# A group mix done with seven products of block sums instead of eight plain products, on Trainium2

## The chip, the core and the metric

The kernel runs on one core of a Trainium2 chip. In the profile PE is the matrix engine (a matmul streams a moving operand of up to 128x512 against a stationary 128x128 operand), PEld the loading of that stationary operand, DVE the vector engine, ACT the scalar engine, POOL the general engine, and SP the engine that issues most transfers. Each engine works through its own instructions in the order in which they stand in the program, and they wait for one another through semaphores. The metric is the device time in microseconds (us), the median of several runs.

## What is computed

One layer of a bidirectional encoder, 1024 tokens of 2048 channels in float32: a normed and modulated input, one combined projection, windowed attention and a pooling branch side by side, each gated, then merged and projected out. The part at issue is the pooling branch. Its 1024 channels fall into four groups of 256; group g averages over a centred window of 2, 4, 8 or 16 tokens, subtracts the token, and is mapped by a 256x256 matrix of its own:

```python
for gi, w in enumerate(POOL_SIZES):                       # 2, 4, 8, 16
    outs.append((cs[:, hi, gi] - cs[:, lo, gi]) / cnt - ug[:, :, gi])
pooled = jnp.stack(outs, axis=2)
mixed = jnp.einsum('bsgc,gcd->bsgd', pooled, w_grp)       # 256x256 per group
y_p = mixed * scale * silu(gate_p)
```

## The kernel before, in words

Every float32 operand is split into a rounded high part (`hi`, written by ACT, line 96) and the rest (`lo`, written by DVE, line 97). A product is then three matmuls: hi with hi, hi with lo, lo with hi. The split is the work that a product asks of ACT and DVE before PE can start.

The large projections use seven products of block sums for a 2x2 block multiplication, in place of eight (`strassen`, line 212). A pair is one such unit: 256 output channels by 1024 tokens. Its seven products are called by their moving operands B11, T3, T2, B21, T4, T1, B22, and they accumulate in three banks X, V and Z: B11 starts X, which ACT copies into Z (line 293); T3 starts V, and DVE reads V into a tile `p` as soon as T3 has ended; T2 and later T1 and B22 add to Z; B21 adds to X; T4 adds to V. A product is 12 matmuls (line 237): four contraction blocks with `whi` and the high moving part, four with `whi` and the low one, four with `wlo`. `whi` and `wlo` are the split weights, four buffers each, made fresh for each product out of a `raw` tile that a transfer brings. DVE also makes the weight sums in `raw` and `ws`, and adds `part` tiles, which hold an earlier half of the sum and are fetched from DRAM.

A pair is a generator of seven steps. `run` (line 347) and `next_pair` (line 1293) walk through it, and at the steps named in `every` they call one entry of a queue `side`. So the pooling branch is recorded between the steps of nine pairs, and its instructions stand among those of the projections. The order written down this way is an input of a scheduler, which then fixes the order of each engine's instructions by its own estimates, except for those that are pinned with `keep`. PE may hence take matmuls of the next product before the last four of the one that it is in.

In the pooling branch `window` (line 1461) works on 128 channels: it loads `u`, adds shifted copies (one to four times, over 1025 to 1039 columns, tiles `win`), corrects the columns at the two edges one by one (line 1478: 1, 3, 7 or 15 of them), forms the mean minus the token over 1024 columns (line 1480), and splits the result into `phi` and `plo`. `mix` (line 1489) makes 128 output channels: two banks of 512 tokens with 6 matmuls each (lines 1509 to 1511), each read out by DVE with scale and gate (line 1512). For each group the queue holds two windows and two mixes; with one first fetch this makes 17 entries, called at the steps 2 and 5 of nine pairs. A group's weights are split once, in 512 columns (`wgh`, `wgl`).

## Time and profile before

| | |
|---|---|
| median of 3 runs | 2086.41 us (2085.77 to 2087.27) |
| the profiled execution's own time | 2088.67 us |
| its span in the profile | 2086.9 us |
| PE, DVE, ACT busy | 2070.1, 1556.7, 1111.0 us (99%, 75%, 53%) |
| first and last transfer of `u` issued | 1190.4 and 1320.2 us |
| first and last matmul of the mixes | 1229.4 and 1376.5 us |

The span is that of one execution. It is 1.8 us shorter than that execution's own time, which was 2.3 us above the median. A row of the timeline gives the start, the length, the engine, the line, and what is written from what; an instruction can start before the one ahead of it has ended, so the distance from start to start says how long the engine is held, and not the length. A group's row gives its count, its busy time, the mean length of one, and the idle time in front of it.

### The profile page before, as it was taken

The page shows a single profiled execution, that of the slowest core. Times are in us where ns is not written, and L with a number is a line of the kernel's source. Part 1 is how long each engine was busy: PE and PEld are TensorE (multiplying, and loading weights), DVE is VectorE, ACT ScalarE, POOL GpSimd, SP SyncE. Part 2 cuts the span into 40 slices and gives each one's busy share as a digit, 9 for nine tenths or more (in the row PEclk, how much of TensorE's full clock was granted, in tenths as well). Part 3 has the DMA queues.
Part 4 walks back from the last instruction along what each step waited for, and adds up shares of the span by engine and source line. Part 5 has one row for each costly group of instructions (what it writes and reads, how often), then busy time and mean ns, then how long its engine had stood idle before and what let it go on. Part 6 is the DMA issues. An engine that isn't in the chain of part 4 may idle for free.

```text
span 2086.9 us, 29056 instructions
## 1 busy us (share of the span) xinstructions
PE 2070.1 (99%) x9524; PEld 1702.2 (82%) x9524; DVE 1556.7 (75%) x2805; ACT 1111.0 (53%) x2121; POOL 42.6 (2%) x143
## 2 busy tenths in 40 slices
PE   8999999999999999999999999999999999999998
PEld 6678887888888888888888888888888788888886
DVE  5889677776565876777777688857867977889667
ACT  5764444444564634666665444334645644767554
POOL 1100000001000000000000000010000000000000
PEclk9999999999999999999999999999999999999999
DMA  9978877887675477645554576675754566786897
GB/s 343 355 270 267 282 240 245 282 284 223 198 232 170 156 250 258 208 164 174 182 170 149 186 233 222 208 239 187 232 175 158 176 201 202 225 305 207 297 334 247
DMA packets 303393, 476.62 MB, mean 228 GB/s; under 512 B 24322, under 2 KB 140650, under 8 KB 303240
## 3 DMA queue, kind: packets, MB, share of 16 engines
q1 hardware_dynamic: 297616, 459.89, 67.2%
q0 software_dynamic: 4560, 12.75, 1.6%
q10 hardware_dynamic: 1064, 2.11, 0.3%
q8 instruction: 75, 1.23, 0.3%
q14 instruction: 78, 0.64, 0.1%
HBM read 346.70 MB, written 130.05 MB: 228 GB/s over the span
## 4 chain that ended last, share of the span: by engine, by line
PE 91%; DMA 4%; DVE 3%; ACT 1%; issue 1%; SPq 0%; DVEq 0%; ACTq 0%; POOL 0%; POOLq 0%
PE Z L237 30%; PE V L237 20%; PE X L237 20%; PE Z L1686 2%; PE Z L1688 2%; PE Z L1687 2%; PE PB L822 1%; PE X L1686 1%; PE X L1687 1%; PE X L1688 1%; PE V L1687 1%; PE V L1686 1%; PE V L1688 1%; DMA raw<-in_w_in_dram 1%; PE PT L1396 1%
## 5 line engine op out<-in xcount | busy, mean ns | idle before, releaser
L96 ACT ACTIVATE whi<-raw 128x512 fp32r<-128x512 f32 (+1 forms) x528 | 314.7, 600 | 482.8 <-PE Z L237 235.2
L97 DVE TENSOR_TENSOR wlo<-raw,whi 128x512 fp32r<-128x512 f32 (+1 forms) x528 | 339.7, 649 | 144.5 <-PE Z L237 110.9
L97 DVE TENSOR_TENSOR wlo<-wr,whi 128x512 fp32r<-128x512 f32 x224 | 150.7, 689 | 51.5 <-ACT whi L96 46.0
L96 ACT ACTIVATE whi<-wr 128x512 fp32r<-128x512 f32 x224 | 138.2, 628 | 86.9 <-DVE wlo L97 29.8
L103 DVE TENSOR_TENSOR raw<-raw,raw 128x512 f32<-128x512 f32 x76 | 52.5, 690 | 92.7 <-DMA raw<-in_w_merge_dram 62.6
L96 ACT ACTIVATE whi<-ws 128x512 fp32r<-128x512 f32 (+1 forms) x88 | 53.0, 602 | 72.2 <-PE X L237 60.8
L237 PE MATMUL Z<-B22h,whi 128*128 128x512 f32 x328 | 89.9, 392 | 0.0
L237 PE MATMUL Z<-T2h,wlo 128*128 128x512 f32 x328 | 88.9, 390 | 0.8 <-DVE wlo L97 0.8
L237 PE MATMUL Z<-T1h,whi 128*128 128x512 f32 x328 | 89.6, 390 | 0.0
L237 PE MATMUL X<-B11h,whi 128*128 128x512 f32 x328 | 89.5, 391 | 0.0
L237 PE MATMUL X<-B21h,whi 128*128 128x512 f32 x328 | 89.5, 391 | 0.0
L237 PE MATMUL V<-T3h,whi 128*128 128x512 f32 x328 | 89.4, 391 | 0.0
L237 PE MATMUL V<-T4h,whi 128*128 128x512 f32 x328 | 89.3, 391 | 0.0
L237 PE MATMUL Z<-T2h,whi 128*128 128x512 f32 x328 | 89.0, 390 | 0.3 <-ACT Z L293 0.2
L237 PE MATMUL X<-B11l,whi 128*128 128x512 f32 x328 | 89.2, 390 | 0.0
L237 PE MATMUL Z<-T1l,whi 128*128 128x512 f32 x328 | 89.0, 390 | 0.0
L237 PE MATMUL Z<-B22l,whi 128*128 128x512 f32 x328 | 88.9, 390 | 0.0
L237 PE MATMUL V<-T3l,whi 128*128 128x512 f32 x328 | 88.9, 390 | 0.0
L237 PE MATMUL X<-B21l,whi 128*128 128x512 f32 x328 | 88.8, 390 | 0.0
L237 PE MATMUL V<-T4h,wlo 128*128 128x512 f32 x328 | 88.8, 390 | 0.0
L237 PE MATMUL X<-B11h,wlo 128*128 128x512 f32 x328 | 88.8, 390 | 0.0
L237 PE MATMUL V<-T4l,whi 128*128 128x512 f32 x328 | 88.8, 390 | 0.0
(421 smaller groups left out, 4908.7 us busy)
## 6 DMA issues: line engine op xcount, KB each, us to landing
part<-part_d SPq DMA_DIRECT2D x136, 256.0 KB, 5.0
ada<-in_w_ada_dram SPq DMA_DIRECT2D x128, 256.0 KB, 5.4
raw<-in_w_merge_dram SPq DMA_DIRECT2D x64, 512.0 KB, 5.4
wr<-ws_dS SPq DMA_DIRECT2D x60, 512.0 KB, 5.4
raw<-in_w_in_dram SPq DMA_DIRECT2D x56, 512.0 KB, 4.1
wr<-in_w_out_dram SPq DMA_DIRECT2D x48, 512.0 KB, 5.0
proj_d<-part SPq DMA_DIRECT2D x68, 256.0 KB, 2.3
sw<-in_w_out_dram SPq DMA_DIRECT2D x64, 256.0 KB, 4.9
```

Source lines behind the costliest of these rows:

```text
L96: ins = (nc.scalar.activation(hi, src, AF.Copy), nc.vector.tensor_tensor(lo, src, f32(hi), ALU.subtract))
L97: nc.vector.tensor_tensor(lo, src, f32(hi), ALU.subtract))
L103: return (eng or nc.vector).tensor_tensor(o, a, b, ALU.add)
L237: nc.tensor.matmul(ps, w_[:, i], op[mov][j][m_], start=fresh and i == 0 and n == 0, stop=i == nj - 1 and n == 2, skip_group_check=True)
L822: keep(nc.tensor.matmul(opened[i, blk], w[:, kh, nt * P:(nt + 1) * P], mov[kh][m], start=j == n == 0, stop=j == 1 and n == 5, skip_group_c ...
L1396: nc.tensor.transpose(pt[:, i * P:(i + 1) * P], p[:, i * P:(i + 1) * P], ident)
L1686: nc.tensor.matmul(pb, hi, w[0], start=first, stop=False, skip_group_check=True)
L1687: nc.tensor.matmul(pb, lo, w[0], start=False, stop=False, skip_group_check=True)
L1688: nc.tensor.matmul(pb, hi, w[1], start=False, stop=last, skip_group_check=True)
```

## The change

The mix of a group becomes a 2x2 block multiplication with seven products, as the pairs have it. The two windows of a group give the four blocks of 128 channels by 512 tokens, the group's matrix four blocks of 128x128. Each product is three matmuls (hi-hi, hi-lo, lo-hi), so a group has 21 where it had 24. DVE makes the sums of the blocks and of the weights, each product has operands split for it alone (512 columns for `phi` and `plo`, 128 for `wgh` and `wgl`), ACT copies three banks per group, and two more additions join the results. X and V are taken from the banks called "at", Z from those called "sc". Since products add to a bank that ACT has written, two matmuls open these banks once (`open_banks`).

The steps of a group are now: its first window and its fetches (called at the end of the group before), then `window` of the second half with `first`, then `second`, `third`, `fourth`, `fifth`. That makes 21 entries over the same nine pairs, at the steps (2, 5), (1, 3, 5), (2, 5) in turn.

```diff
-            u = pp.tile([P, S + 2 * PAD], F32, tag="u", name=f"u{i}")
+            u = pp.tile([P, S + 2 * PAD], F32, tag="u", name=f"u{i}", bufs=2)
...
-            nc.vector.scalar_tensor_tensor(win, win, 1.0 / w, u[:, PAD:PAD + S],
-                                           op0=ALU.mult, op1=ALU.subtract)
-            hi = pp.tile([P, S], F32R, tag="phi", name=f"phi{i}", bufs=2)
-            lo = pp.tile([P, S], F32R, tag="plo", name=f"plo{i}", bufs=2)
-            split(hi, lo, win)
-            pooled[i] = (hi, lo)
+            nc.vector.scalar_tensor_tensor(mid_, win, 1.0 / w, mid_, op0=ALU.mult, op1=ALU.subtract)
+            blocks[j] = mid_[:, 0:512], mid_[:, 512:1024]
-        def mix(g, j):
...
-            for s in range(2):
-                sl = slice(s * 512, (s + 1) * 512)
-                ps = bank("at")
-                for k in range(2):
-                    hi, lo = pooled[2 * g + k]
-                    nc.tensor.matmul(ps, gh[:, k, wn], hi[:, sl], start=k == 0, stop=False)
-                    nc.tensor.matmul(ps, gh[:, k, wn], lo[:, sl], start=False, stop=False)
-                    nc.tensor.matmul(ps, gl[:, k, wn], hi[:, sl], start=False, stop=k == 1)
...
+            def operand(name, src):
+                ops[name] = [pp.tile([P, 512], F32R, tag=t, name=uid(t), bufs=4) for t in ("phi", "plo")]
+                split(*ops[name], src)
+            def weight(name, src):
+                wts[name] = [pp.tile([P, P], F32R, tag=t, name=uid(t), bufs=3) for t in ("wgh", "wgl")]
+                split(*wts[name], src)
+            def product(name, to, fresh=False):
+                (wh, wl), (mh, ml) = wts.pop(name), ops.pop(name)
+                for n, (w_, m_) in enumerate(((wh, mh), (wh, ml), (wl, mh))):
+                    nc.tensor.matmul(banks[to], w_, m_, start=fresh and n == 0, stop=n == 2, skip_group_check=True)
...
+            def first():
+                (b11, b12), (b21, b22) = blocks[0], blocks[1]
+                st["a"] = a11, a21, a12, a22 = [st["raw"][:, kh, n * P:(n + 1) * P] for kh in range(2) for n in range(2)]
+                sub(b12, b12, b11)
+                t2, st["p7"] = spare("t2")
+                st["u2"], _ = spare("u2")
+                sub(t2, b22, b12)
+                operand("B11", b11)
+                weight("B11", a11)
+                sub(b11, t2, b11)
+                operand("T3", b11)
+                s3 = pp.tile([P, P], F32, tag="wgs", name=uid("wgs"))
+                sub(s3, a11, a21)
+                weight("T3", s3)
+                add(a21, a21, a22)
+                sub(a11, a21, a11)
+            def second():
+                product("B11", "X", True)
+                nc.scalar.activation(banks["Z"], banks["X"], AF.Copy)
+                weight("T2", a11)
+                operand("T2", t2)
+                product("T3", "V", True)
+                nc.scalar.activation(st["p7"], banks["V"], AF.Copy)
+                weight("B21", a12)
+                operand("B21", b21)
+                sub(b21, b21, t2)
...
+            def third():
...
+                product("T2", "Z")
+                nc.scalar.activation(st["u2"], banks["Z"], AF.Copy)
...
+                product("B21", "X")
+                result("11", banks["X"])
...
+            def fourth():
...
+                product("T4", "V")
+                add(st["u2"], banks["V"], st["u2"])
+                result("21", st["u2"])
+                product("T1", "Z")
+                add(st["p7"], banks["Z"], st["p7"])
+                result("22", st["p7"])
...
+            def fifth():
+                product("B22", "Z")
+                result("12", banks["Z"])
+                for n, sg in enumerate(st["sg"]):
+                    store(yp_d[(2 * g + n) * P:(2 * g + n + 1) * P, :], sg)
+                then()
+        def open_banks():
+            hi = op["B11"][0][0]
+            for _ in range(2):
+                nc.tensor.matmul(bank("sc", "OPEN"), hi[:, 0:P], hi, start=True, stop=True)
...
-        while side:
-            next_pair((2, 5))
+        for n in range(9):
+            next_pair((1, 3, 5) if n % 3 == 1 else (2, 5))
```

The change leaves the instructions of the projections as they are, but the scheduler places them anew among those of the mixes. Three places follow. In the names a number marks the buffer; a name that comes back with the same number is the same tile.

The first place is PE in the last group (window 16), where the pair's product B22 adds to Z. Before, the twelve matmuls stand together; these are the last two with the high weights and the four with `wlo`, and the next product follows:

```order
L237 MATMUL Z_13084<-B22l_7073,whi_13323 128x512
L237 MATMUL Z_13084<-B22l_7077,whi_13323 128x512
L237 MATMUL Z_13084<-B22h_7064,wlo_13324 128x512
L237 MATMUL Z_13084<-B22h_7068,wlo_13324 128x512
L237 MATMUL Z_13084<-B22h_7072,wlo_13324 128x512
L237 MATMUL Z_13084<-B22h_7076,wlo_13324 128x512
L237 MATMUL Z_13284<-T2h_6899,whi_13375 128x512
```

With the change the same place reads:

```order
L237 MATMUL Z_13250<-B22l_7073,whi_13548 128x512
L237 MATMUL Z_13250<-B22l_7077,whi_13548 128x512
L1503 MATMUL X_13587<-phi_13527,wgh_13531 128x512
L1503 MATMUL X_13587<-plo_13528,wgh_13531 128x512
L1503 MATMUL X_13587<-phi_13527,wgl_13532 128x512
L237 MATMUL Z_13250<-B22h_7064,wlo_13549 128x512
L237 MATMUL Z_13250<-B22h_7068,wlo_13549 128x512
L237 MATMUL Z_13250<-B22h_7072,wlo_13549 128x512
L237 MATMUL Z_13250<-B22h_7076,wlo_13549 128x512
L237 MATMUL Z_13456<-T2h_6899,whi_13568 128x512
```

A product of the group's mix (line 1503) now stands between the eight matmuls with the high weights and the four that need `wlo_13549`.

The second place is DVE at the same point. Before, from the last windowing additions on (V_13085 is the bank that T4 has just added to, V_13285 that of the next pair's T3):

```order
L103 TENSOR_TENSOR win_8_13351<-win_4_13349 128x1025
L103 TENSOR_TENSOR u_2651_13179<-V_13085,u_2651_13179 128x512
L97 TENSOR_TENSOR wlo_13324<-raw_13073,whi_13323 128x512
L1478 TENSOR_SCALAR win_8_13351<-win_8_13351 128x1 x15
L106 TENSOR_TENSOR raw_13271<-raw_13271 128x4x128
L1480 SCALAR_TENSOR_TENSOR win_8_13351<-win_8_13351,u_13341 128x1024
L103 TENSOR_TENSOR p_2644_13121<-p_2644_13121,u_2658_13267 128x512
L97 TENSOR_TENSOR wlo_13376<-raw_13271,whi_13375 128x512
L97 TENSOR_TENSOR plo_13370<-win_8_13351,phi_13369 128x1024
```

With the change (V_13457 is the bank of the next pair's T3):

```order
L103 TENSOR_TENSOR p_2765_13493<-V_13457,part_13447 128x512
L103 TENSOR_TENSOR win_4_13503<-win_2_13501 128x1033
L97 TENSOR_TENSOR wgl_13532<-wg_13417,wgh_13531 128x128
L103 TENSOR_TENSOR win_8_13505<-win_4_13503 128x1025
L97 TENSOR_TENSOR wgl_13543<-wgs_13540,wgh_13542 128x128
L1478 TENSOR_SCALAR win_8_13505<-win_8_13505 128x1 x15
L106 TENSOR_TENSOR wg_13417<-wg_13417 128x128
L1480 SCALAR_TENSOR_TENSOR u_13495<-win_8_13505,u_13495 128x1024
L97 TENSOR_TENSOR wlo_13549<-raw_13239,whi_13548 128x512
L106 TENSOR_TENSOR t_2766_13524<-u_13495,u_13389 128x512
L106 TENSOR_TENSOR raw_13443<-raw_13443 128x4x128
```

The `wlo` of B22, which stood ahead of the edge columns and of the read of the next V, now stands behind both.

The third place is PE in the group before it (window 8), in the pair's product T1. Before, it is twelve matmuls in a row; these are its last two with the high weights, then three of the four with `wlo`:

```order
L237 MATMUL Z_12698<-T1l_7038,whi_12855 128x512
L237 MATMUL Z_12698<-T1l_7042,whi_12855 128x512
L237 MATMUL Z_12698<-T1h_7029,wlo_12856 128x512
L237 MATMUL Z_12698<-T1h_7033,wlo_12856 128x512
L237 MATMUL Z_12698<-T1h_7037,wlo_12856 128x512
```

With the change, the last rows ahead of the same matmuls are:

```order
L237 MATMUL V_13048<-T3l_6892,whi_13068 128x512
L237 MATMUL V_13048<-T3l_6896,whi_13068 128x512
L1503 MATMUL X_13104<-phi_12993,wgh_12997 128x512
L1503 MATMUL X_13104<-plo_12994,wgh_12997 128x512
L1503 MATMUL X_13104<-phi_12993,wgl_12998 128x512
L237 MATMUL Z_12808<-T1h_7029,wlo_13015 128x512
L237 MATMUL Z_12808<-T1h_7033,wlo_13015 128x512
```

Between T1's eight matmuls with `whi_13014` and its four with `wlo_13015` there now stand the first eight of the next pair's B11, the first eight of its T3, and a product of the mix: 19 matmuls.

## Prediction

> **What bounds the kernel now.** I read the page's busy times first, then PE's waits, then the stretch in which the pooling branch runs, engine by engine.

> ```profile
> span 2086.9 us, 29056 instructions
> PE 2070.1 (99%) x9524; PEld 1702.2 (82%) x9524; DVE 1556.7 (75%) x2805; ACT 1111.0 (53%) x2121; POOL 42.6 (2%) x143
> ```

> The waits of PE over the whole run, longest first, hold one row on the split weights:

> ```profile
> PE Z L237 <- DVE wlo L97: 0.8, 1, 0.8
> ```

> PE never stops for long, so the end is set by the number of matmuls, as long as DVE delivers in time. The stretch of the mixes, by engine, and what DVE waits for in it (us in total, times, longest):

> ```profile
> core 0: us, PE busy (x) PEld busy (x) DVE busy (x) ACT busy (x) POOL busy (x), PEclk, DMA share, GB/s
> 1190.00:1378.00 188.00, 188.00 (x829) 155.30 (x828) 150.84 (x257) 72.51 (x108) 2.73 (x18) 1.00 0.69 221
> ```
> ```profile
> DVE raw L103 <- DMA raw<-in_w_merge_dram: 18.0, 8, 4.3
> DVE win L103 <- DMA u<-proj_d: 5.1, 4, 2.1
> DVE p L103 <- DMA part<-part_d: 1.3, 1, 1.3
> ```

> PE is full. DVE is busy for 150.84 of 188 us (80%), and of its 37.2 idle us 24.4 are waits for transfers. It is ahead of PE: here PE's timeline in the last group,

> ```profile
> 1348.52 1.07 PE L237 MATMUL V<-T3h,wlo 128*128 128x512 f32 x4
> 1349.43 1.07 PE L237 MATMUL Z<-B22h,whi 128*128 128x512 f32 x4
> 1350.34 1.07 PE L237 MATMUL Z<-B22l,whi 128*128 128x512 f32 x4
> 1351.24 1.07 PE L237 MATMUL Z<-B22h,wlo 128*128 128x512 f32 x4
> ```

> and DVE's just before:

> ```profile
> 1338.02 1.23 DVE L103 TENSOR_TENSOR win<-win 128x1033 f32<-128x1033 f32 x1
> 1339.17 0.68 DVE L103 TENSOR_TENSOR part<-X,part 128x512 f32<-128x512 f32 x1
> ...
> 1340.37 1.22 DVE L103 TENSOR_TENSOR win<-win 128x1025 f32<-128x1025 f32 x1
> 1341.50 0.69 DVE L103 TENSOR_TENSOR u<-V,u 128x512 f32<-128x512 f32 x1
> 1342.11 0.69 DVE L97 TENSOR_TENSOR wlo<-raw,whi 128x512 fp32r<-128x512 f32 x1
> 1342.70 0.99 DVE L1478 TENSOR_SCALAR win<-win 128x1 f32<-128x1 f32 x15
> 1343.62 0.68 DVE L106 TENSOR_TENSOR raw<-raw 128x512 f32<-128x512 f32 x1
> 1344.21 1.22 DVE L1480 SCALAR_TENSOR_TENSOR win<-win,u 128x1024 f32<-128x1024 f32 x1
> 1345.35 0.68 DVE L103 TENSOR_TENSOR p<-p,u 128x512 f32<-128x512 f32 x1
> 1345.95 0.68 DVE L97 TENSOR_TENSOR wlo<-raw,whi 128x512 fp32r<-128x512 f32 x1
> ```

> The `wlo` of 1342.11 (wlo_13324 of the quoted order) ends at 1342.80 and is used at 1351.24: 8.4 us of lead. From start to start these rows give what holds an engine: a matmul 0.227 us (2.72 for the twelve from 1348.52 to 1351.24); on DVE 0.60 for 512 columns, 1.15 for 1033, 1.13 for 1025, 0.92 for 15 edge columns, 1.14 for the 1024 of line 1480. Two narrow rows give 0.20 for 128 columns:

> ```profile
> 1186.60 0.48 DVE L1418 TENSOR_TENSOR g<-PV,g 128x128 f32<-128x128 f32 x2
> 1186.91 0.80 SPq L1421 DMA_DIRECT2D ya_d<-g  x2
> 1187.00 0.68 DVE L106 TENSOR_TENSOR raw<-raw 128x512 f32<-128x512 f32 x1
> ```

> **The change, part by part.** PE first. The mixes are three rows of 32 matmuls:

> ```profile
> L1509 PE MATMUL b<-phi,wgh 128*128 128x512 f32 x32 | 12.5, 390 | 0.0
> ...
> L1510 PE MATMUL b<-plo,wgh 128*128 128x512 f32 x32 | 12.5, 390 | 0.0
> L1511 PE MATMUL b<-phi,wgl 128*128 128x512 f32 x32 | 12.5, 390 | 0.0
> ```

> 96 become 84 and two that open banks: ten fewer, 10 x 0.227 = **2.3 us saved**.

> DVE gains 28 `plo`, 16 block subtractions and 8 additions of 512 columns and loses four `wgl`: net 48 x 0.60 = 28.8. It gains 44 of 128 columns (8.8) and loses eight `plo` of 1024 (9.1). Together 28.5 us on 150.8, in a stretch that shrinks to 185.7: 97% busy. On average that still fits, by 6.4 us, but only if the waits for transfers vanish as DVE falls back and no read of a bank lies in the wrong place. ACT gains 36 of 512 columns net of `wgh`, 28 narrow ones, and loses eight wide ones; even at 0.63 us for all 64 that is 40 on 72.5 of 188, so ACT hides it. Transfers keep number and size.

> The sum is therefore made where the windows are widest, since a group's two windows now follow each other directly.

> *Group with window 16, B22.* In the quoted order `p_2765<-V_13457` cannot start before T3 has ended, and `wlo_13549` stands eight rows behind it. DVE from the start of the one to the end of the other: 0.60 + 1.15 + 0.20 + 1.13 + 0.20 + 0.92 + 0.20 + 1.14 + 0.68 = 6.2 us. PE has 11 matmuls between T3's end and that `wlo` (eight of B22 and three of the mix): 2.5 us. DVE starts some 0.2 later than PE goes on, since a matmul ends 0.39 after its start and the next starts after 0.227. So PE stops for 6.2 + 0.2 - 2.5 = 3.9 us, and once released it has to load the weights, which nothing now covers:

> ```profile
> L1509 PEld LDWEIGHTS b<-phi,wgh x32: 187/188/188, 1229.2 to 1375.8; 128*128 128x128 f32 x32
> ```

> 0.2 more: **4.1 us**. This is a floor, as any lateness of DVE at T3's end adds to it.

> *Just behind it, T2.* `raw_13443` follows two rows later; its end is 1.2 us after the end of `wlo_13549`, ACT's `whi_13568` takes 0.6 on it and the weights 0.2, while PE has four matmuls (0.9, started 0.2 late): **0.9 us**.

> *Group with window 8, T1.* From `p_2646<-V_12809`, the read behind T3, to `wlo_13015` the change's order has 29 rows on DVE: twelve of 512 columns (7.2), three reads with gate (2.0; the `sil` row below), six window additions (6.9), two of line 1480 (2.3), two rows of seven edge columns (0.8, at the 0.06 a column of the fifteen), three narrow ones (0.6), and the last `wlo` (0.7): 20.5 us.

> ```profile
> L1512 DVE SCALAR_TENSOR_TENSOR sil<-b,cols,sil 128x512 f32<-128x512 f32 x16 | 11.8, 748 | 3.0 <-PE b L1511 2.6
> ```

> PE has 84 matmuls in between (65 up to T1's eighth, three products of the mix among them, then the 19 that now stand ahead of T1's rest): 19.0 us. So the stop is 20.5 + 0.2 - 19.0 = 1.7 if DVE is free and `part` is there when T3 ends; a late `part` (1.3 in its row above) makes it 3.0. I take 2.6 with half of that added, and 0.2 for the weights: **2.8 us**.

> *Groups with windows 2 and 4.* For window 4, T1's rest has nine rows of 512 columns, one read with gate, two window additions, one of line 1480, edges, three narrow rows and its own `wlo` behind T3, 11.0 us, against 59 matmuls (13.4): 2 us of cover, so nothing, or up to 1.5 if `raw` or `part` come as late as in their rows. That stays for the range.

> *The clock.* In the last slices the granted clock falls after the last matmul, and at the start the same matmul takes 618 ns on average until 9.95 us, and 391 later:

> ```profile
> 2078.50 0.39 PE L1688 MATMUL Z<-wlo,mh 128*128 128x512 f32 x1
> ```
> ```profile
> 2081.00:2082.00 1.00, 0.00 (x0) 0.00 (x0) 1.00 (x3) 0.00 (x0) 0.00 (x0) 0.83 0.00 0
> 2082.00:2083.00 1.00, 0.00 (x0) 0.00 (x0) 1.00 (x2) 0.00 (x0) 0.00 (x0) 0.50 0.98 361
> ```
> ```profile
> L528 PE MATMUL GEMV<-ada,scz 128*32 128x256 f32 x16 | 3.6, 618 | 0.3 <-DMA ada<-in_w_ada_dram 0.3
> L528 PE MATMUL GEMV<-ada,scz 128*32 128x256 f32 x8 | 1.0, 391 | 0.0
> ```

> Full clock until about 2081.7, half after: 2.8 us behind the end of the last matmul (2078.9). A stop of 4.1 us is longer, so I count on the drop. Recovery took 3.6 us of matmuls at half speed, which costs 1.8 us; T2's wait of 0.9 vanishes in it, since PE then comes later: **0.9 us net**.

> [...]

> **Sum:** -2.3 + 2.8 + 4.1 + 0.9 + 0.9 = +6.4 us. The span of 2086.9 becomes 2093.3; the median of the runs, 2086.41, becomes **2092.8 us**.

> **The rivals.**
> 1. *DVE keeps its lead; faster.* Then only the ten matmuls count: 2084.1. For it: 37.2 us of idle DVE against 28.5 of new work. Against it: it decides only if `wlo_13549` is ready within 2.5 us of T3's end, and the rows ahead of it hold DVE for 6.2.
> 2. *Half of it.* If transfers come early, window 8 costs nothing, and the clock stays up: -2.3 + 4.1 + 0.9 = +2.7, 2089.1; between that and 2090.6 it is hardly told from no change.
> 3. *Late transfers too.* DVE's waits for `raw` (2.25 us on average) and `u` stay although DVE is late, each straight on PE: 1.5 in window 4, another 1.5 each in windows 8 and 16, the clock down in window 8 too (1.8): 6.4 + 6.3 = +12.7, 2099.1; with half of that 2096.
> 4. *The clock holds* through the stop, as no row shows a stop of this length in the middle of the run: -2.3 + 2.8 + 4.1 + 0.9 = +5.5, 2091.9, inside the forecast's range.

> That the change doesn't do what it says is excluded by the order: 86 matmuls stand where 96 did.

> **How the numbers follow.** The forecast with rival 4 gets 0.60, its own range 2090.6 to 2095.5; late transfers 0.18; half of it 0.14; DVE in time 0.08. The range leaves out the faster case (0.08) and the far end of the late one: 2089 to 2098. A measurement tells about 0.2%, 4.2 us: faster means below 2082.2, which needs more than the ten matmuls: 0.04. Same (2082.2 to 2090.6) takes the rest of that case and most of "half": 0.16. Slower: 0.80.

> **What would show it.** PE's waits in the changed profile name `wlo` of Z, T1's before B22's, 1.5 to 3.5 and about 4 us long, in the last two groups, and none in the first. DVE is busy for over 175 us of the stretch. The granted clock is below 1 in a slice of a few us behind the longer stop. I am wrong if `wlo` is ahead of PE there, if the waits name a transfer or ACT instead, or if PE also stops at the mixes' own operands.

## The result, and the profile after

The changed kernel takes 2101.17 us (median of 6 runs, 2099.08 to 2105.22) against 2086.84 for the kernel before beside it (6 runs): a ratio of 1.0064, with an interval of 1.0054 to 1.0075. Slower, by the prediction's own bound of 0.2%, was right; 2092.8 was too little, and 2098 too low an end of the range. The profiled execution took 2100.37 us. The head of its page, and the waits of PE over the whole run (us in total, times, longest):

```profile
span 2098.6 us, 29186 instructions
PE 2071.4 (99%) x9514; PEld 1701.2 (81%) x9514; DVE 1583.4 (75%) x2889; ACT 1126.7 (54%) x2177; POOL 42.6 (2%) x143
```
```profile
PE Z L237 <- DVE wlo L97: 6.6, 4, 3.7
...
PE X L1503 <- DVE wgl L97: 1.4, 1, 1.4
PE V L237 <- DVE u L103: 1.1, 2, 0.8
```

The row on `wlo` has grown from 0.8 to 6.6 us, and PE waits for two more products of DVE; of the wait for `u`, 0.8 us stand at 259.5 us, far ahead of the mixes. The stretch of the mixes, with the columns that the prediction's row has:

```profile
1190.00:1390.00 200.00, 191.84 (x829) 156.74 (x828) 177.69 (x341) 89.42 (x165) 1.41 (x13) 0.98 0.64 207
```

PE idles for 8.2 of 200 us, DVE works for 177.7, and the clock is 0.98 on average. Where it happens, from PE's timeline of the changed kernel:

```profile
1304.78 0.39 PE L1503 MATMUL X<-phi,wgl 128*128 128x512 f32 x1
1307.56 1.19 PE L237 MATMUL Z<-T1h,wlo 128*128 128x512 f32 x4 [2.39 <-DVE wlo L97]
...
1316.17 1.21 PE L237 MATMUL Z<-T2h,wlo 128*128 128x512 f32 x4 [0.36 <-DVE wlo L97]
...
1352.38 1.07 PE L237 MATMUL V<-T3h,wlo 128*128 128x512 f32 x4
...
1355.77 0.50 PE L1503 MATMUL X<-plo,wgh 128*128 128x512 f32 x1 [0.28 <-DVE plo L97]
1357.71 0.50 PE L1503 MATMUL X<-phi,wgl 128*128 128x512 f32 x1 [1.44 <-DVE wgl L97]
1361.90 2.07 PE L237 MATMUL Z<-B22h,wlo 128*128 128x512 f32 x4 [3.69 <-DVE wlo L97]
...
1368.46 0.40 PE L1503 MATMUL V<-phi,wgh 128*128 128x512 f32 x1
...
1421.94 1.15 PE L237 MATMUL V<-T3h,whi 128*128 128x512 f32 x4 [0.27 <-DVE u L103]
```

In the group with window 8 PE stops for 2.75 us at T1's and T2's `wlo`; in that with window 16 for 5.41 us, 1.44 of it at the mix's own weights and 3.69 at B22's `wlo`; behind the branch for 0.27. After the longest stop come 16 matmuls in 6.56 us (1361.90 to 1368.46); at 0.227 us each, as at the full clock, they would make 3.63. DVE in the same place:

```profile
1333.01 0.69 DVE L103 TENSOR_TENSOR raw<-raw,raw 128x512 f32<-128x512 f32 x1 [3.19 <-DMA raw<-in_w_merge_dram]
...
1355.63 0.68 DVE L103 TENSOR_TENSOR p<-V,part 128x512 f32<-128x512 f32 x1
...
1361.16 0.68 DVE L97 TENSOR_TENSOR wlo<-raw,whi 128x512 fp32r<-128x512 f32 x1
```

From the read of V to the end of B22's `wlo` are 6.2 us, the sum that the prediction made. But T3 had ended at 1353.45, and DVE came to the read 2.2 us later. It had been busy since a `raw` tile arrived at 1333.0, with one wait of 0.75 us, for a `wg` that came at 1337.0. In the group with window 8 the read behind T3 and T1's `wlo` (the first of the two in its row) are:

```profile
1287.02 0.69 DVE L103 TENSOR_TENSOR p<-V,part 128x512 f32<-128x512 f32 x1 [0.75 <-DMA part<-part_d]
...
1306.82 1.28 DVE L97 TENSOR_TENSOR wlo<-raw,whi 128x512 fp32r<-128x512 f32 x2
```

T3 had ended at 1286.13 there, so DVE was 0.9 us late, at a `part` that it waited for.

**A measure with less noise than the run's time.** In every pair T4's last four matmuls have a row of their own, in all these kernels. From the first such row of the stretch to the twelfth behind it (before 1190.39 to 1441.11 us, changed 1192.81 to 1453.76) lies all of the changed work. The table splits that stretch at the sixth, eighth and tenth such row; the columns hold about the groups with windows 2 and 4, that with 8, that with 16, and the pairs behind (in e7, which has the groups in another order, they are only the same stretches of the pairs). All in us, each from one profile.

| kernel | 2 and 4 | 8 | 16 | behind | sum |
|---|---|---|---|---|---|
| before | 106.35 | 43.62 | 43.63 | 57.12 | 250.72 |
| before, second profile (e5) | 106.29 | 43.62 | 43.63 | 57.12 | 250.66 |
| changed | 105.17 | 45.56 | 51.90 | 58.32 | 260.95 |
| changed, second profile (e1) | 105.18 | 45.80 | 50.14 | 59.18 | 260.30 |
| changed, third profile (e8) | 105.17 | 46.62 | 50.40 | 58.56 | 260.75 |
| all windows 2 (e2) | 105.17 | 42.99 | 42.84 | 58.55 | 249.55 |
| window 16 made 2 (e6) | 105.18 | 46.38 | 42.84 | 59.19 | 253.59 |
| window 8 made 2 (e9) | 105.18 | 42.76 | 49.98 | 59.01 | 256.93 |
| stop filled (e3) | 105.18 | 46.57 | 49.73 | 59.16 | 260.64 |
| four rows more, window 16 (e10) | 105.17 | 45.89 | 52.32 | 59.61 | 262.99 |
| four rows more, window 2 (e11) | 105.50 | 47.44 | 50.32 | 59.28 | 262.54 |
| window additions on GpSimd (e4) | 112.71 | 48.88 | 52.88 | 58.86 | 273.33 |
| other order (e7, groups 16, 8, 2, 4) | 106.87 | 42.15 | 42.85 | 57.80 | 249.67 |

The stretch of the kernel before repeats within 0.1 us, and the groups 2 and 4 within 0.01 wherever they are unchanged. The changed kernel loses 9.6 to 10.2 us in it, all behind those two groups.

### The profile page after: what moved, and what is told of

The parts are those of the page before. It is cut to its first block, busy times and chain, and to the rows that moved or that the text cites. A ratio compares the mean times of both kernels' runs of the same rounds, so it can differ in the third digit from the quotient of the medians.

```text
span 2098.6 us, 29186 instructions
## 1 busy us (share of the span) xinstructions
PE 2071.4 (99%) x9514; PEld 1701.2 (81%) x9514; DVE 1583.4 (75%) x2889; ACT 1126.7 (54%) x2177; POOL 42.6 (2%) x143
## 4 chain that ended last, share of the span: by engine, by line
PE 87%; DVE 5%; DMA 5%; issue 1%; ACT 1%; SPq 0%; POOL 0%; DVEq 0%; ACTq 0%; POOLq 0%
PE Z L237 28%; PE V L237 18%; PE X L237 18%; PE Z L1765 2%; PE Z L1766 2%; PE Z L1767 2%; PE PB L822 2%; DMA raw<-in_w_merge_dram 1%; PE V L1765 1%; PE X L1766 1%; PE X L1765 1%; PE V L1766 1%; PE X L1767 1%; PE V L1767 1%; DVE wlo L97 1%
## 5 line engine op out<-in xcount | busy, mean ns | idle before, releaser
L97 DVE TENSOR_TENSOR wlo<-raw,whi 128x512 fp32r<-128x512 f32 (+1 forms) x528 | 338.9, 649 | 141.9 <-PE Z L237 107.9
L97 DVE TENSOR_TENSOR wlo<-wr,whi 128x512 fp32r<-128x512 f32 x224 | 150.2, 688 | 51.2 <-ACT whi L96 48.2
L103 DVE TENSOR_TENSOR raw<-raw,raw 128x512 f32<-128x512 f32 x76 | 52.4, 690 | 80.6 <-DMA raw<-in_w_merge_dram 48.0
L237 PE MATMUL Z<-B22h,wlo 128*128 128x512 f32 x328 | 89.7, 393 | 3.7 <-DVE wlo L97 3.7
L237 PE MATMUL Z<-T1h,wlo 128*128 128x512 f32 x328 | 88.8, 390 | 2.4 <-DVE wlo L97 2.4
L237 PE MATMUL V<-T3h,whi 128*128 128x512 f32 x328 | 89.6, 392 | 1.1 <-DVE u L103 1.1
L237 PE MATMUL Z<-T2h,whi 128*128 128x512 f32 x328 | 89.9, 393 | 0.4 <-ACT Z L293 0.2
L237 PE MATMUL X<-B11h,whi 128*128 128x512 f32 x328 | 89.7, 391 | 0.5 <-DVE part L103 0.5
L237 PE MATMUL Z<-B22h,whi 128*128 128x512 f32 x328 | 89.9, 392 | 0.0
L237 PE MATMUL Z<-T2h,wlo 128*128 128x512 f32 x328 | 89.2, 391 | 0.5 <-DVE wlo L97 0.5
L237 PE MATMUL X<-B21h,whi 128*128 128x512 f32 x328 | 89.5, 391 | 0.0
L237 PE MATMUL Z<-T2l,whi 128*128 128x512 f32 x328 | 89.5, 392 | 0.0
L237 PE MATMUL Z<-T1h,whi 128*128 128x512 f32 x328 | 89.5, 390 | 0.0
L237 PE MATMUL V<-T4h,whi 128*128 128x512 f32 x328 | 89.4, 391 | 0.0
L237 PE MATMUL X<-B11l,whi 128*128 128x512 f32 x328 | 89.2, 390 | 0.0
L237 PE MATMUL Z<-B22l,whi 128*128 128x512 f32 x328 | 88.9, 390 | 0.0
L237 PE MATMUL X<-B21l,whi 128*128 128x512 f32 x328 | 88.9, 390 | 0.0
L237 PE MATMUL V<-T3l,whi 128*128 128x512 f32 x328 | 88.9, 390 | 0.0
L237 PE MATMUL X<-B11h,wlo 128*128 128x512 f32 x328 | 88.9, 390 | 0.0
```

The source lines that it names most:

```text
L97: nc.vector.tensor_tensor(lo, src, f32(hi), ALU.subtract))
L103: return (eng or nc.vector).tensor_tensor(o, a, b, ALU.add)
L237: nc.tensor.matmul(ps, w_[:, i], op[mov][j][m_], start=fresh and i == 0 and n == 0, stop=i == nj - 1 and n == 2, skip_group_check=True)
```

## The experiments

**e1, e8: the changed kernel again.** No edit.

> The changed kernel once more, nothing edited. Profiled once its span was 11.7 us above the kernel before, while the median of its six runs is 14.3 above. Theory A (the stops at T1's and B22's `wlo` are the whole of it, and what varies from run to run is how late DVE stands when T3 ends, with the transfer of `raw` behind it): the second profile has the same two places, window 8 and window 16, with stops that sum to 8 to 13 us, and the span moves by what the stops and the half-speed clock move. Rival B (the runs lose the rest elsewhere, outside the pooling stage): the stops are as in the first profile within 0.5 us, and the span differs by more than 1 us.

> The changed kernel for a third profile. Theory A: T1's stop 2.3 to 2.7 us, B22's 3.6 to 3.8 behind wgl's 1.4, in the same places, since they follow from DVE's rows; what differs is the clock: a drop behind B22's stop of 3.4 to 6.8 us at half speed, in some runs one behind T1's stop too (1.7 us more). Stretch 260 to 263 us. Rival B (the stops vary with the transfers by more than 1 us): other lengths of the stops at a clock that holds.

2102.17 us against 2088.22 before (ratio 1.0077, 1.006 to 1.0095), and a single time of 2101.75. The stops stand at the same places and are nearly the same: T1's 2.61 and 2.53 us, B22's 3.68 twice; only `wgl` ahead of it varies, 1.45 and 0.91, where e8 expected 1.4. That fits DVE's rows as what sets them. What differs is the clock: in e1 it is low only behind B22's stop (at 0.50 for 3.4 us from 1357.98), in e8 behind both (3.4 us from 1306.26, 6.8 from 1357.46). Theory A holds within the stretch, but the sign of e1's rival B came as well: the stops differ by less than 0.5 us (the one at `u` apart), while the span is 1.8 us shorter, and PE reaches the stretch at 1189.50 us instead of 1192.81. Theory A does not give the time of the runs, which lies 11 to 16 us above before (first comparison) for a stretch that costs 10.

**e5: the kernel before again.** No edit.

> The kernel before once more, nothing edited, for a second profile. From the T4 rest of the pair ahead of the mixes to that of the twelfth pair behind it the first profile took 250.72 us (1190.39 to 1441.11), the changed kernel's two took 260.95 and 260.30. Theory A (that stretch is steady, and the 2 to 4 us by which the runs of the changed kernel exceed its stretch's loss are drawn elsewhere, as the start's half-speed clock): 250.7 within 0.3 again, with the time up to the stretch other than 1190.4 by 1 to 3 us. Rival B (the stretch itself varies in the kernel before as well): 252 or more.

250.66 us: the stretch is steady, as theory A had it, and the other half of that theory failed here, since the time up to the stretch was 1190.26, the same again.

**e2, e6, e9: narrow windows.**

```diff
 e2
-                window(g, POOLS[g], 0)
+                window(g, 2, 0)
 (and the same for the second window; e6: 2 only for g == 3, e9: 2 only for g == 2)
```

> All four groups take windows of width 2, so the averages over 4, 8 and 16 are left out (the output is not the reference's); the seven products, the splits, the reads of banks, the pairs and the transfers stay as they are. DVE loses twelve window additions in all (2 x (1+2+3) at about 1.15 = 13.8 us) and 52 edge columns (about 3.1 us). Theory A (DVE's rows of the wide windows stand between T3's end and the `wlo` that PE needs): the stop in the last group goes and the clock stays up, at most about 1 us is left in the group before, and the time is 2084 to 2087. Rival B (it is the reads of banks and splits of the seven products themselves, or late transfers, that make DVE late): the stops stay, 2096 to 2101.

> Only the last group takes windows of width 2 in place of 16 (its wide averages are left out, so the output is not the reference's); groups 2, 4 and 8 as in the changed kernel. Theory A (each stop belongs to its own group's windows): B22's stop in the last group and the clock's drop behind it vanish, T1's in the group before stays at about 2.5 us with T2's 0.3; of the stretch's loss of 9.6 to 10.2 us some 2 to 3 are left, 252.5 to 253.5 us, and the time is about 8 us less than the changed kernel's. Rival B (DVE carries its lateness on from group to group, so the last group still stops): 256 to 259.

> The mirror of the run before: only the group with window 8 takes windows of width 2 (its wide averages are left out, so the output is not the reference's); the last group keeps width 16. Theory A (DVE comes late into the last group because of the group before it, which holds its buffers and so the loads of `raw` back): T1's stop is at most 1.1 us, and in the last group DVE reaches the read of T3's bank without delay; B22's stop with that at `wgl` ahead of it falls from 4.6 to 5.1 us to about 4, the blocks of the last group from 50.1-51.9 to 48.5-49.5 us. Theory B (the last group's own rows and its own `raw` are all that counts): both stops there as before, 4.6 to 5.1 us. Under both the rest of the loss is the clock, 1.7 us at half speed for 3.4 or 3.4 for 6.8.

With all windows narrow the stretch takes 249.55 us, 1.17 less than before, with two short stops left in PE's timeline:

```profile
1303.22 1.19 PE L237 MATMUL Z<-T1h,wlo 128*128 128x512 f32 x4 [0.53 <-DVE wlo L97]
...
1411.24 1.15 PE L237 MATMUL V<-T3h,whi 128*128 128x512 f32 x4 [0.51 <-DVE u L103]
```

Without them it would be 2.2 us shorter than before, which is the ten matmuls. The seven products themselves, with their splits and reads, can hence be had at almost no cost to PE. (The edge columns that go are 44, 2.6 us, and not the 52 of the expectation.) But narrow windows change more than the amount of work: the scheduler then puts B22's `wlo` ahead of the read of V, with no product of the mix between its matmuls, and only five matmuls between T1's eighth and its `wlo` instead of 19. So these runs show that the stops go with the wide windows, and don't separate their rows from the order that they bring. The run's time did not show the gain: 2090.38 us, ratio 1.0009 (0.9999 to 1.0018), above the 2084 to 2087 expected.

With only window 16 made narrow, its block falls to the same 42.84 us and the one of window 8 stays (stop 2.43, the clock at 0.50 for 3.4 us from 1304.42). The stretch, 253.59 us, comes out at the end of the 252.5 to 253.5 expected; the time, 2095.56 us, ratio 1.0031 (1.002 to 1.0043), is 6.6 us below e1's and not 8. With only window 8 made narrow, T1's stop falls to 0.29, and the last group keeps its stops, 1.41 and 3.68; 2097.6 us, ratio 1.0041 (1.0026 to 1.0057). So each stop belongs to its own group, and theory B of e9 is right: DVE doesn't carry its lateness in from the group before. There too it waited 4.1 us for a `raw` at 1327, was then busy nearly throughout, and read V 1.6 us after T3's end. In e6 the read came 1.9 us late and cost nothing, as the `wlo` stood ahead of it.

**e10, e11: the same four rows of DVE at two places.**

```diff
+            if w == 16 and j == 1:        # e11: w == 2
+                for _ in range(4):
+                    nc.vector.tensor_tensor(win[:, 0:512], win[:, 0:512], win[:, 0:512], ALU.max)
             for e in list(range(w // 2)) + list(range(S - w // 2 + 1, S)):
```

> Four additions to DVE's work, rows of 512 columns (0.60 each, 2.4 us) that change nothing in the values, in the second window of width 16, between T3's read and B22's `wlo`. Theory A (PE has no cover left there): all 2.4 us fall on PE; B22's stop with that at `wgl` grows from 4.6 to 5.1 to 7.0 to 7.5 us, and the last group's two blocks from 50.1-51.9 to 52.5-55. Rival B (DVE makes it good behind, as the loads wait for it less): less than 1 us.

> The same four rows in the second window of the group of width 2 instead. Theory A (there DVE is ahead of PE, so work counts only where the window is wide): nothing, at most 0.5 us, in the groups 2 and 4, whose blocks took 105.17 us in all three profiles of the changed kernel, and the stops of the later groups as they were. Rival B (DVE is at its limit over the whole stretch, 97% busy, and every row more is paid, wherever it stands): 2.4 us more in the stretch.

In the group with window 2 they cost 0.33 us (105.50 against 105.17); so DVE is not at its limit over the whole stretch. The sum of e11 is larger mainly by a low clock in window 8 (0.50 for 3.4 us from 1307.86), which e8 has too; a stop of 0.35 us at `plo` there stands in no other profile here, and whether the four rows brought it isn't shown. In the group with window 16, PE's and then DVE's timeline of e10:

```profile
1355.64 0.50 PE L1506 MATMUL X<-phi,wgl 128*128 128x512 f32 x1 [1.09 <-DVE wgl L97]
1361.11 2.08 PE L237 MATMUL Z<-B22h,wlo 128*128 128x512 f32 x4 [4.97 <-DVE wlo L97]
```
```profile
1360.37 0.68 DVE L97 TENSOR_TENSOR wlo<-raw,whi 128x512 fp32r<-128x512 f32 x1
1360.97 1.22 DVE L1483 SCALAR_TENSOR_TENSOR u<-win,u 128x1024 f32<-128x1024 f32 x1
```

B22's stop grows by 1.28 us, from 3.69. That is less than the 2.4 expected, and DVE's timeline says why: the scheduler put this `wlo` ahead of the 1024-column row of the window (line 1480 in the changed kernel) instead of behind it, so that 4 x 0.60 came in ahead of it and 1.14 went behind. The difference is 1.26; from the read of V to the end of the `wlo` DVE takes 7.50 us instead of 6.21, and that falls on B22's stop one for one. With the stop at `wgl`, which varies by itself, it is 6.06 us against 4.6 to 5.1 in the other profiles, short of the 7.0 to 7.5 expected, and the block of 52.32 stays just under the 52.5 expected. The single times are 2103.57 and 2101.13 us.

**e3: the stop filled.** Sixteen matmuls more, whose results are overwritten.

```diff
                 product("B11", "X", True)
+                if g == 3:
+                    mov = op["B11"][0][0]
+                    for _ in range(16):
+                        keep(nc.tensor.matmul(banks["V"], mov[:, 0:P], mov, start=True, stop=True, skip_group_check=True))
```

> Sixteen matmuls more, whose results are overwritten, between the mix product ahead of B22's `wlo` and that `wlo` in the last group: 16 x 0.227 = 3.6 us of PE's work. Theory A (PE stands there for about 4 us waiting for DVE, and the clock falls in the stop): the sixteen fit into the stop, the clock stays at 1.00, and the time is 2 to 3 us less than the changed kernel's, 2098 to 2099. Rival B (PE's stop is no idle time that can be used, or the clock doesn't depend on it): 3.6 us more, about 2104.8. Rival C (the stop is filled, and the lower clock cost nothing since PE had to wait for DVE anyway): the same as the changed kernel within 0.7.

PE's timeline at that place:

```profile
1359.77 0.50 PE L1503 MATMUL X<-phi,wgl 128*128 128x512 f32 x1 [1.44 <-DVE wgl L97]
1360.11 3.81 PE L1545 MATMUL V<-B11h 128*128 128x512 f32 x16
1363.96 1.21 PE L237 MATMUL Z<-B22h,wlo 128*128 128x512 f32 x4
```

They fit into the stop, and the clock stays at 1.00 there. With 3.6 us of matmuls more, the last group's block is 0.4 to 2.2 us shorter than in the three profiles of the changed kernel. The run's time, 2101.43 us (ratio 1.0061, 1.0049 to 1.0074), is above the 2098 to 2099 of A and can't tell A from C. What the trace does show is that the low clock had cost something, and that rival B's 3.6 us did not come.

**e4: the window additions on GpSimd.**

```diff
-                add(nxt[:, lo_:hi_], cur[:, lo_ - d0:hi_ - d0], cur[:, lo_ + d1:hi_ + d1])
+                add(nxt[:, lo_:hi_], cur[:, lo_ - d0:hi_ - d0], cur[:, lo_ + d1:hi_ + d1], nc.gpsimd)
```

> The twenty shifted additions of the windows go from DVE to GpSimd, nothing else. DVE loses 20 x 1.15 = 23 us of its 177.7 in the stretch, and most of what stood ahead of T1's and B22's `wlo`. How long GpSimd takes for 128x1033 no row of this kernel shows. Theory A (DVE's lateness is the whole loss): no stop at `wlo`, 2083 to 2086, faster than the kernel before by up to the ten matmuls. Rival B (GpSimd takes the window so slowly that `mid_` comes late and the mixes' own operands stop PE, or the two engines slow each other): over 2090, with PE's waits naming `phi`, `plo` or DVE's naming POOL.

2112.4 us, ratio 1.0118 (1.0104 to 1.0131): 10 us slower than the changed kernel. Groups of POOL by shape, then DVE's waits, in the stretch; then DVE's and POOL's timelines of one place:

```profile
L103 POOL TENSOR_TENSOR win<-u 128x1039 f32<-128x1039 f32 x8 | 19.0, 2376 | 60.6 <-issue 31.4 <-DMA u<-proj_d 28.9
```
```profile
DVE win L1478 <- POOL win L103: 6.8, 2, 3.8
```
```profile
1306.60 0.74 DVE L1508 SCALAR_TENSOR_TENSOR sil<-Z,cols,sil 128x512 f32<-128x512 f32 x1
1307.26 1.74 DVE L106 TENSOR_TENSOR u<-u 128x512 f32<-128x512 f32 x1
1308.92 2.39 DVE L97 TENSOR_TENSOR plo<-u,phi 128x512 fp32r<-128x512 f32 x1
1311.23 0.68 DVE L103 TENSOR_TENSOR part<-X,part 128x512 f32<-128x512 f32 x1
```
```profile
1306.22 4.54 POOL L103 TENSOR_TENSOR win<-win 128x1037 f32<-128x1037 f32 x2 [1.23 <-DVE u L1480]
```

One addition of 1039 columns takes GpSimd 2.4 us where it took DVE 1.24. While it runs here, DVE's rows that read two operands and no bank are held too: 2.39 and 1.74 us for 512 columns instead of 0.68, and 0.68 again when POOL is done; the row of 1306.60, which reads the bank Z, took its 0.74. Beside POOL's row of 1240.39, which itself took 3.71 us, three such rows kept their length (0.29 for 128 columns, 0.68 twice for 512). So DVE was not relieved: over the whole run it has twenty rows fewer and is busy for 1585.8 us, against 1583.4 in the changed kernel. The lengthened rows make what stands behind them late: PE waits 7.7 us in all for `part`, 5.1 of it for the row of 1311.23 shown here, and 4.3 for a `p` that stands nine us behind DVE's longest wait for POOL. Theory A fell, rival B holds, though PE stops longer at the pairs' `part` and `p` than at the mixes' operands that it named.

**e7: all the work in another order.** Wide windows first, each second window a step of its own, other places in the same nine pairs.

```diff
-        for g in reversed(range(len(POOLS))):
+        for g in reversed((3, 2, 0, 1)):
...
-            side.extendleft(reversed([lambda g=g, first=steps_[1]: (window(g, POOLS[g], 1), first())] + list(steps_[2:])))
+            side.extendleft(reversed([lambda g=g: window(g, POOLS[g], 1)] + list(steps_[1:])))
...
-        for n in range(9):
-            next_pair((1, 3, 5) if n % 3 == 1 else (2, 5))
+        for every in ((1, 3, 6), (1, 3, 5), (2, 6), (1, 3, 6), (1, 3, 5), (1, 3, 6), (2, 6), (1, 4, 6), (1, 3, 6)):
+            next_pair(every)
```

> The changed kernel with all its work, otherwise ordered: the groups in the order 16, 8, 2, 4, each second window as a side step of its own (25 steps), at other places in the same nine pairs. DVE's sum of work is the same 177 us. Theory A (the loss is the order, not the amount: wide windows behind a read that PE waits for): stops of about 1 us in the first pair, none behind, the clock at 1.00 throughout; stretch 249.5 to 251.5 us, 9 to 10 us under the changed kernel, and within 0.2% of the kernel before. Rival B (DVE has too much work in 186 us wherever it stands, with transfers behind it): stops of 4 us or more in all, 254 to 260.

The stretch by engine, and all of PE's stops in it:

```profile
1190.00:1390.00 200.00, 199.11 (x876) 163.94 (x875) 182.71 (x350) 92.45 (x172) 2.51 (x15) 1.00 0.67 217
```
```profile
1215.81 1.20 PE L237 MATMUL X<-B11h,wlo 128*128 128x512 f32 x4 [0.28 <-DVE wlo L97]
1223.34 1.20 PE L237 MATMUL Z<-T2h,whi 128*128 128x512 f32 x4 [0.61 <-ACT whi L96]
```

DVE is busy for 182.7 of 200 us, more densely than in the changed kernel, and PE idles for 0.9. The stretch takes 249.67 us, 11 less than the changed kernel and 1.05 less than before; the time is 2089.7 us, ratio 1.0001 (0.9992 to 1.001). So it was the order and not the amount of DVE's work that cost the time. The order of the groups, the side steps and the places were changed together; which of them does it was not tried singly. In this order the whole change is worth about 1 us, which the time can't tell from no change; no kernel here beats the one before measurably.

## Why the prediction was wrong in size and right in kind

**The ten matmuls, -2.3:** right. All windows narrow, the stretch is 2.2 us shorter than before, stops set aside.

**Groups 2 and 4, nothing:** right; their block is 1.2 us shorter.

**Window 8, T1's `wlo`, 2.8:** right, in its parts too. From the read to the end of the `wlo` DVE takes 20.5 us, as counted, and `part` made it 0.9 us late where the sum had allowed half of 1.3. The sum itself has a slip: 1.7 and half of 1.3 make 2.35 and not 2.6, so its own terms give 2.55. The stop is 2.39, with 0.36 at T2 behind it; 2.61 with 0.30 in e1; 0.29 in e9.

**Window 16, B22's `wlo`, 4.1: this step failed.** DVE's 6.2 us from the read of V to the end of the `wlo` were right to the tenth. But the sum let DVE be at that read when T3 ends, called the result a floor, and added nothing. DVE came 2.2 us late in the first profile, 1.1 to 1.7 in e1, e8, e9, e10 and e11, since it had rows almost without a gap from the last `raw` on, which arrived 20 us before T3's end. PE's stop follows that lateness: 5.41, 5.13, 5.09, 4.69 and 4.59 us where DVE was 2.18, 1.73, 1.59, 1.17 and 1.10 late (changed kernel, e1, e9, e11, e8), so 3.2 to 3.5 are left for a DVE in time, where the sum had 3.9. B22's own part is 3.68 or 3.69 in all five; the lateness stood at the mix's own operands, 1.44 us of it at `wgl` in the first profile, which the prediction named as something that would prove it wrong. The count should have begun at the last transfer that DVE waits for, not at the bank that it reads. What would happen if that `raw` came earlier was not tried.

**The clock, 0.9 with T2's 0.9:** that it falls was right, and so was that T2's wait vanishes in it; the size lay between those measured. It fell around B22's stop in all six profiles that have this stop (the changed kernel, e1, e8, e9, e10, e11). Windows of 1 us, the changed kernel and then e1 (granted clock third from the end):

```profile
1360.00:1361.00 1.00, 0.00 (x0) 0.00 (x0) 1.00 (x2) 0.51 (x2) 0.00 (x0) 0.96 0.00 0
1361.00:1362.00 1.00, 0.10 (x1) 0.10 (x1) 1.00 (x3) 0.00 (x0) 0.00 (x0) 0.50 0.00 0
...
1367.00:1368.00 1.00, 1.00 (x5) 0.78 (x4) 1.00 (x3) 0.69 (x1) 0.00 (x0) 0.63 0.00 0
```
```profile
1357.00:1358.00 1.00, 0.00 (x0) 0.00 (x0) 1.00 (x2) 0.14 (x1) 0.00 (x0) 0.99 0.00 0
...
1361.00:1362.00 1.00, 1.00 (x5) 0.81 (x4) 1.00 (x2) 1.00 (x3) 0.00 (x0) 0.80 0.69 237
```

Reading 0.50 as the floor, it was at half speed from 1360.92 to 1367.74, 6.8 us, and in e1 from 1357.98 to 1361.40, 3.4 us. The first costs 2.9 us (16 matmuls in 6.56 instead of 3.63), the second 1.6, against 1.8 for the two terms together. I had one length, 3.6 us, from the start of the run (an estimate from the length of the matmuls, 618 ns and then 391: the granted clock itself reads 1.00 in those slices), and took the fall from the stop's length alone, which does not decide it (last section).

**Not in the sum at all:** a stop at `u` behind the branch (0.27 us, 1.11 in e1), ahead of which DVE had waited 5.7 us for a `raw` in the first profile, and a clock that falls in window 8 too, in four profiles of seven (to 0.50, for 3.4 us each).

**The sum** for the changed kernel's profile: -2.2 + 2.75 + 5.41 + 2.93 + 0.27 = 9.2 of the 10.2 us; the other 1.0 lies in starts behind the stops and gaps too short for a row, as far as I can place it. The failed step is 1.3 us of the 3.8 by which the stretch lost more than the 6.4 predicted, the clock 1.1. The stretch alone would have left the time inside the range (2086.84 + 10.2 = 2097.0); the rest lies outside it, and the prediction had nothing there.

**The rivals.** DVE in time, and half of it, are excluded by the stops; the clock did not hold. "Late transfers too" was nearest in time (2099.1), and its part on the clock in window 8 came in four profiles of seven. But window 4 lost nothing, and PE stopped directly for no `raw` and no `u` of the branch; a late `raw` and a late `part` only made DVE late. It got 0.18.

**What stays open.** The median rose by 14.3 us (interval 11.3 to 15.7), the stretch by 10. Outside the stretch PE takes 1828.2 and 1827.7 us up to the end of its last matmul in the two profiles of before, and 1827.5 to 1833.6 in the eleven profiles of kernels with seven products, 1829.7 on average. Two of those eleven, e2 and e3, lost 2.5 to 3 us at the very start, where the same matmuls took longer. PE's timeline of the same eight matmuls, in before and then in e2:

```profile
11.98 1.04 PE L491 MATMUL XT<-ident,xt 128*128 128x128 f32 x8
```
```profile
12.00 1.92 PE L491 MATMUL XT<-ident,xt 128*128 128x128 f32 x8
```

The code there is the same in both kernels, and two profiles of before are too few to say how often it draws this. The matmuls of 512 columns take 0.63 to 0.80 us up to the one that starts at 17.84 us in e2 and at 18.37 in e3, and 0.39 to 0.50 behind it; in before, the changed kernel, e1 and e4 they take 0.39 to 0.50 from the first one on. That a low clock lengthened them is an estimate from these lengths, as the granted clock reads 1.00 in those slices. The changed kernel's first profile lost its time elsewhere: PE idles there for 10.0 us ahead of the stretch, in e1 and e8 for 7.6 and 7.4, in before for 7.5 and 7.6, and up to the branch PE, DVE and ACT run the same rows in the same order in before and in the changed kernel. So of the 14.3 us, 11.7 are the difference of the two profiled executions: 10.2 in the stretch, 1.3 in the rest up to PE's last matmul and 0.2 behind that. The other 2.6 come from the executions themselves: before's profiled one was 1.8 us above its median, the changed kernel's 0.8 below. Whether what stands outside the stretch is more than chance isn't settled.

## What to carry to other kernels

Count an in-order engine's rows back from the operand that the bound engine will need to the last point at which the engine is known to be free, often a transfer, and compare with the work of the bound engine over the same span; an average load says neither that it fits nor that it doesn't (91% busy with 0.9 us of stops in e7, 89% with 8.2 in the changed kernel). The same four rows cost 0.33 us beside a narrow window, and beside a wide one what they added ahead of the operand fell on the bound engine one for one; so where a schedule allows it, put the largest side work where the lead is greatest before counting saved matmuls as gain. A stretch between two landmarks that all variants share repeats within 0.1 us where nothing stops the bound engine, and within 0.7 in the changed kernel, where the time of a run tells 2.

## What the runs showed of the hardware

```profile
1311.00:1312.00 1.00, 0.04 (x1) 0.04 (x1) 1.00 (x5) 0.00 (x0) 0.00 (x0) 0.74 0.00 0
...
1359.00:1360.00 1.00, 1.00 (x4) 0.76 (x5) 1.00 (x13) 0.00 (x0) 0.95 (x1) 0.64 0.38 143
...
1376.00:1377.00 1.00, 0.54 (x1) 0.50 (x2) 1.00 (x3) 1.00 (x2) 0.00 (x0) 0.67 0.94 327
```

It falls at 1311.48, 1359.28 and 1376.34 us: 47.80 and 17.06 apart, 14 and 5 steps. A stop of 2.4 to 2.6 us in window 8 brought the fall in four profiles (e3, e6, e8, e11) and none in three (the changed kernel, e1, e10), by how it lay against the steps, laid from the falls: in e6 2.20 us of the step that ends at the fall were idle (64%), in the changed kernel 1.13 and 1.26 in two neighbouring steps, and it held. In the stretch of all thirteen profiles every step that ended in a fall had at least 1.82 us idle (53%, in e4), and no other step at full clock more than 1.51 (44%, in the changed kernel). The two lengths go by the same steps: when PE came back 0.98 us into a step (changed kernel) the clock stayed low through the next, when 0.41 us in (e1), it came up at the step's end; so it is in all fourteen, with 0.98 us or more for the long ones and at most 0.48 for the short.
